# One block of a two-block language model: the overflow branch of its mixture of experts moved to the last expert

## The chip, the cores and the metric

One core of one Trainium2 chip. The time is device microseconds of one execution; of several executions the median is given. The engines are TensorE (PE in the profile; its weight loads are PEld), VectorE (DVE), ScalarE (ACT), GpSimd (POOL) and SyncE (SP), which here only issues DMAs. Each has its own instruction queue and works through it in order; they wait for each other by semaphores.

## The reference

512 tokens of width 1024 go through a first model of two layers (retention and gated linear attention with a SwiGLU, then an HGRN2 mixer with a mixture of experts) and through a second one of one layer. What matters here is the mixture of experts at the end of the first model:

```python
def moe_swiglu(h, w_router, w_gate, w_up, w_down):
    xt = h.reshape(b * t, d)
    logits = (xt @ w_router).astype(jnp.float32)
    top_logits, top_idx = lax.top_k(logits, TOP_K)          # 2 of 8
    gates = jax.nn.softmax(top_logits, axis=-1)
    ...
    hid = (jax.nn.silu(lax.ragged_dot(xs, w_gate, group_sizes))
           * lax.ragged_dot(xs, w_up, group_sizes))
    ys = lax.ragged_dot(hid, w_down, group_sizes)
    ...
    out = jnp.einsum('nk,nkd->nd', gates.astype(y.dtype), y)
```

with 8 experts, each of a gate and an up matrix of 1024 x 3584 and a down matrix of 3584 x 1024 in float32: some 44 MB an expert.

## The kernel before, in words

`build` runs `mixer_ab`, `ffn`, `mixer_c` (first model), `moe`, then `mixer2` and `peer` (second model). The residual `h` stays in SBUF as four tiles of 128 tokens.

**Slots.** Experts are taken in order of how many tokens they have; the place e has a fixed number of slots, `CAPS` = 152, 152, 144, 136, 132, 128, 124, 120. Expert 0 of the weights is always taken first (its key is the largest, from `iota8`), the other places' expert numbers are computed and stand in `eid`. Tokens that find no slot go a second, slower way, `moe_overflow` (L1196): it is a branch on the value `anyo`, and with these inputs it is skipped.

**The entry**, `moe` from L856 on. `moe_ranks` (L1088) takes the router's logits, finds the two best experts of each token, counts with matmuls against a triangular matrix how many tokens stand before it (`pr`, L1111), and works out on VectorE, in some thirty small instructions, the places, the flags `anyo` and `flags`, the overflow rank `rk` and the row `pos` of each token in the DRAM buffer `xg`. Then `values_load` (L878) brings `anyo` into a register of every engine, and `tc.If` (L879) holds the overflow path. `moe_route` (L1178) follows: it makes `first`, for each token tile a 128 x 152 table with the token's scale at its slot with the first expert (L1183; it lies in the tile `hid2`, which the overflow path also writes), scales the token rows (`xn`, L1190), scatters them on POOL to `xg` (eight indirect DMAs, L1065), and computes the gates. `prep_first` (L895) gathers the first expert's tokens by a matmul of `h` with `first` (L900; so it need not wait for the scatters), 8 times over 128 columns, and `split` (L888) makes of each result a high part, a bfloat16 copy (ACT) and a low part (VectorE).

**The experts**, L929 on. Each has 14 chunks of gate and up: `wload_b` (L1052) loads 1 MB on SP (L1055), ACT makes the high part `wh` (L1057), VectorE the low part `wl` (L1058); then per 128 columns a group of 8 matmuls with `wh` (L960) and 8 with `wl` (L962), so four groups a chunk. The down matrix comes in 16 loads (L994, L998). Raw weights lie in five buffers, three of the pool `wraw` and two of a second pool, taken in turn; the overflow path loads its weights into `wraw` too. High and low parts have four buffers, two from each of two pools, which the overflow path does not use. Four PSUM tiles (`mm`) hold the sums until ACT and VectorE have taken them out (L963, L964). The last expert's results are added to `h` at once, with a selection matmul; the others are stored to `yg` by ACT (L1027, L1029) and gathered at the end. `prep(e + 1)` (L904) loads the next expert's token rows from `xg` on ACT's queue (L908, and L911 for the rows beyond 128 where there are any: experts 1 to 4) and transposes them while expert e runs.

**The order in each queue** is not that of the program. The tile framework's scheduler lays the instructions out by program order and by when they will be ready; the whole `tc.If` is placed as one piece, and instructions that share no tile with it may go to either side. `issue_after` puts VectorE instructions behind given ones: here all VectorE work of the first expert behind `first`. A tile name in a pool stands for as many buffers as `bufs` says, used in turn; a new tile waits for the users of the old one, those inside the `tc.If` too.

## Time and profile before

| | us |
|---|---|
| median of 3 runs (lowest, highest) | 3930.39 (3926.33, 3931.0) |
| the profiled execution, its own time | 3932.15 |
| its span, from the first to the last instruction | 3930.4 |
| TensorE busy in the span | 3732.5 (95%) |
| VectorE | 2859.0 (73%) |
| ACT | 2122.3 (54%) |
| mixture of experts, first gather matmul | 1098.07 |
| last expert's first gate and up matmul | 2079.4 |

Mean granted clock of TensorE: 0.969. Times in the views are microseconds from the start of the span. In a timeline a row gives start, duration, engine, line, operation, what is written and read, how many instructions are merged, and in brackets how long the engine had been idle and what ended that. In the table of stretches a row gives the stretch, its length, the busy time (and instructions) of PE, PEld, DVE, ACT and POOL, the granted clock of TensorE as a share of 2.4 GHz, the busy share of the DMA rings and their GB/s. An engine's name with a q (SPq, PEldq) is its queue: DMA issues, branches, register loads and semaphore steps.

### The profile page before, as it was taken

The numbers are of one execution on the slowest core, as the hardware profiler recorded it, in microseconds if no ns is written. First come the engines' busy times: TensorE is split into PE (matmuls) and PEld (weight loads), VectorE is DVE, ScalarE is ACT, GpSimd is POOL, SyncE is SP. The second block draws the span as 40 slices with busy tenths as digits, with TensorE's granted clock in tenths as the row PEclk, the third lists the DMA queues.
The fourth block names the chain that finished last, engine by engine and source line by source line (L and its number), as shares of the span: only waits on it lengthen the run. The fifth ranks groups of instructions, "written<-read, shape, count | busy, mean of one in ns | idle before, by whom it ended". The sixth has DMA issues, their size and how long they took to land.

```text
span 3930.4 us, 64830 instructions
## 1 busy us (share of the span) xinstructions
PE 3732.5 (95%) x25823; PEld 3375.3 (86%) x25824; DVE 2859.0 (73%) x4565; ACT 2122.3 (54%) x3418; POOL 587.0 (15%) x364
## 2 busy tenths in 40 slices
PE   8999999999879999999999799998999899999997
PEld 7887888899879999999999787788999899788886
DVE  4655642545478888999999867569997777677777
ACT  4432222555467877888888565533347676333333
POOL 0000000000010000000000200002335656233333
PEclk9999999999989999999999899899999999999999
DMA  4244542212178888899999521126877777989996
GB/s 141 89 126 169 192 156 92 94 66 70 65 260 310 297 320 325 321 348 343 355 331 370 223 72 42 36 104 227 282 251 248 242 267 260 355 337 334 343 343 226
DMA packets 229131, 887.48 MB, mean 226 GB/s; under 512 B 21080, under 2 KB 81769, under 8 KB 176981
## 3 DMA queue, kind: packets, MB, share of 16 engines
q1 hardware_dynamic: 150706, 640.57, 45.5%
q0 software_dynamic: 40608, 146.29, 10.6%
q10 hardware_dynamic: 37507, 96.42, 6.8%
q8 instruction: 204, 3.34, 0.3%
q14 instruction: 106, 0.87, 0.1%
HBM read 810.11 MB, written 71.47 MB: 224 GB/s over the span
## 4 chain that ended last, share of the span: by engine, by line
PE 45%; DVE 12%; issue 6%; DMA 5%; ACT 2%; POOL 2%; SPq 1%; ACTq 0%; POOLq 0%; DVEq 0%
PE mm L960 8%; PE mm L994 5%; PE acc L165 5%; PE acc L167 5%; PE acc L166 5%; PE mm L962 4%; PE mm L998 2%; DVE wl L160 2%; DVE row L1954 2%; DMA G<-gst 2%; DMA row<-in_peer_u_rows,eidx 1%; DVE wl L1058 1%; PE mm L165 1%; PE mm L167 1%; PE mm L166 1%
## 5 line engine op out<-in xcount | busy, mean ns | idle before, releaser
L1058 DVE TENSOR_TENSOR wl<-wraw,wh 128x2048 bf16<-128x2048 f32 (+1 forms) x352 | 772.1, 2196 | 126.2 <-ACT wh L1057 123.4
L1057 ACT ACTIVATE wh<-wraw 128x2048 fp32r<-128x2048 f32 (+1 forms) x352 | 647.6, 1841 | 174.8 <-PE mm L994 65.3
L160 DVE TENSOR_TENSOR wl<-wraw,wh 128x2048 fp32r<-128x2048 f32 (+1 forms) x219 | 511.1, 2334 | 255.3 <-ACT wh L159 253.8
L159 ACT ACTIVATE wh<-wraw 128x2048 fp32r<-128x2048 f32 (+1 forms) x219 | 415.7, 1898 | 474.3 <-PE mm L166 188.1
L960 PE MATMUL mm<-xhl,wh 128*128 128x304 f32 (+6 forms) x3584 | 566.2, 300 | 14.6 <-DVE gate L964 9.7
L960 PEld LDWEIGHTS mm<-xhl,wh 128*128 128x128 f32 x3584 | 475.7, 190 | 20.7 <-DVE gate L964 7.1
L167 PE MATMUL mm<-xh,wl 128*128 128x384 f32 (+1 forms) x1088 | 376.4, 351 | 19.4 <-DVE wl L160 19.1
L165 PE MATMUL mm<-xh,wh 128*128 128x384 f32 (+1 forms) x1088 | 379.9, 351 | 5.5 <-issue 2.2
L166 PE MATMUL mm<-xl,wh 128*128 128x384 f32 (+1 forms) x1088 | 378.6, 348 | 0.0
L1757 POOL DMA_INDIRECT row<-in_peer_u_rows,eidx x128 | 207.2, 1619 | 594.6 <-DVE pv L1781 405.6
L962 PE MATMUL mm<-xb,wl 128*128 128x152 bf16 (+6 forms) x3584 | 292.3, 224 | 0.0
L166 PE MATMUL acc<-wl,ah 128*128 128x512 f32 x768 | 291.9, 396 | 0.0
L167 PE MATMUL acc<-wh,al 128*128 128x512 f32 x768 | 279.5, 396 | 2.9 <-DVE al L2056 2.9
L165 PE MATMUL acc<-wh,ah 128*128 128x512 f32 x768 | 268.2, 396 | 2.8 <-ACT ah L2055 2.8
L994 PE MATMUL mm<-hid,wh 128*128 128x304 f32 (+6 forms) x1792 | 259.3, 296 | 2.0 <-DVE gate L964 2.0
L1757 POOL DMA_INDIRECT row<-in_peer_v,eidx x128 | 192.9, 1507 | 357.8 <-DVE h L1961 309.2
L994 PEld LDWEIGHTS mm<-hid,wh 128*128 128x128 f32 x1792 | 233.6, 190 | 2.6 <-PE mm L962 2.4
L962 PEld LDWEIGHTS <-wl 128*128 128x128 bf16 x3584 | 212.3, 98 | 26.4
L167 PEld LDWEIGHTS mm<-xh,wl 128*128 128x128 f32 x1088 | 210.6, 194 | 26.7 <-DVE wl L160 23.6
L165 PEld LDWEIGHTS mm<-xh,wh 128*128 128x128 f32 x1088 | 211.8, 195 | 10.9 <-issue 2.8
L166 PEld LDWEIGHTS mm<-xl,wh 128*128 128x128 f32 x1088 | 210.9, 194 | 2.8
L1954 DVE CUSTOM_DVE_ANT_0 row<-row,h 128x1024 f32<-128x1024 f32 x128 | 173.7, 1386 | 44.5 <-DMA row<-in_peer_u_rows,eidx 44.4
(597 smaller groups left out, 8138.5 us busy)
## 6 DMA issues: line engine op xcount, KB each, us to landing
wraw<-in_moe_w_gate SPq DMA_DIRECT2D x112, 1024.0 KB
wraw<-in_moe_w_up SPq DMA_DIRECT2D x112, 1024.0 KB
wraw<-in_moe_w_down SPq DMA_DIRECT2D x128, 896.0 KB
wraw<-in_peer_u SPq DMA_DIRECT2D x64, 1024.0 KB
wraw<-in_peer_v SPq DMA_DIRECT2D x64, 1024.0 KB
wraw<-in_w_ada SPq DMA_DIRECT2D x24, 1024.0 KB
G<-gst SPq DMA_DIRECT2D x24, 1024.0 KB
gw<-G ACTq DMA_DIRECT2D x64, 384.0 KB
```

Of the source, the lines that this page charges most:

```text
L159: nc.scalar.activation(wh[:, :n], raw[:, :n], AF.Copy)
L160: nc.vector.tensor_sub(wl[:, :n], raw[:, :n], wh[:, :n].bitcast(F))
L165: mm(out, ah, bh, start=start, stop=False)
L166: mm(out, ah, bl, start=False, stop=False)
L167: mm(out, al, bh, start=False, stop=stop)
L960: nc.tensor.matmul(ps, wh[:, d, fs], xhl[:, d], start=d == 0, stop=False)
L962: nc.tensor.matmul(ps[:, 0], wl[:, d, fs], xb[:, d], start=False, stop=d == ND - 1)
L994: nc.tensor.matmul(ps, wh[:, fs], hid[at[ft][0]][:, at[ft][1]], start=ft == 0, stop=False)
L1057: nc.scalar.activation(wh[:, :n], raw[:, :n], AF.Copy)
L1058: nc.vector.tensor_sub(wl[:, :n], raw[:, :n], wh[:, :n].bitcast(F))
L1757: self.tc.keep_in_program_order(nc.gpsimd.indirect_dma_start(out=r, out_offset=None, in_=table, in_offset=bass.IndirectOffsetOnAxis(ap=eid ...
L1954: nc.vector.tensor_tensor_reduce(r, r, h2, 1.0, 0.0, op0=OP.mult, op1=OP.add, accum_out=dots[:, q:q + 1])
```

## The change

The `tc.If` with the overflow path goes from the entry to the top of the last expert's turn. In front of it the last expert's first two weight loads are issued and split (`ready`). `b0`, `r0` and `first` are made inside `moe_ranks`, straight behind the counting matmuls, in a tile of their own in the pool `moe` (four times 152 floats a partition). The second row tile of `prep` is named `yr2`, so that it shares one buffer with the output tile of that name, which the overflow path uses too. `of_expert` and the load of the expert's number stand a little higher in the loop.

```diff
@@ -873,12 +873,10 @@
             self.open_w(self.mw)
             rstd = ph.tile([128, NT], F, name="mrstd")
             ranks = self.moe_ranks(ph, psum, flags, anyo, rstd, pos)
+            first = ranks.first
             self.mr.close()
             work = c.enter_context(tc.tile_pool(name="moew", bufs=2, reuse_waits="tile"))
-            rv = nc.values_load(anyo[0:1, 0:1], min_val=0, max_val=1)
-            with tc.If(rv > 0):
-                self.moe_overflow(work, psum, h, g, rstd, ranks, flags, xo, yo, yg)
-            done, first = self.moe_route(ph, work, h, ranks, gates, pos, rstd)
+            self.moe_route(ph, work, h, ranks, gates, pos, rstd)
 
             def parts(C):
                 return (work.tile([128, ND * 2 * CAP], FR, name="xhl")[:, :ND * 2 * C].rearrange(
@@ -907,7 +905,7 @@
                 xr = work.tile([128, D], F, name="xr", bufs=1)[:n]
                 ld = [nc.scalar.dma_start(xr, xg[row:row + n])]
                 if C2:
-                    xr2 = work.tile([CAP - 128, D], F, name="xr2", bufs=1)[:C2]
+                    xr2 = work.tile([CAP - 128, D], F, name="yr2", bufs=1)[:C2]
                     ld.append(nc.scalar.dma_start(xr2, xg[row + n:row + C]))
                 for l in ld:
                     for s in self.scatters:
@@ -923,28 +921,35 @@
                 return x
 
             order = ExitStack()
-            for x in done:
+            for x in ranks.done:
                 order.enter_context(tc.issue_after(x.ins))
             ready = self.ready + [self.wload_b(a[n][0, 1], 2048) for n in ("moe_w_gate", "moe_w_up")]
             nxt = prep_first()
             for e in range(NE):
                 if e == 1:
                     order.close()
+                if e:
+
+                    ev = nc.values_load(self.eid[0:1, e:e + 1], engines=(mybir.EngineType.SP,), min_val=0, max_val=NE - 1)
+
+                def of_expert(name, *at):
+                    if e == 0:
+                        return a[name][(0,) + at]
+                    return a[name][(bass.ds(ev, 1),) + at].rearrange("o p c -> (o p) c")
+
+                if e == NE - 1:
+
+                    ready = [self.wload_b(of_expert(n, 0), 2048) for n in ("moe_w_gate", "moe_w_up")]
+                    rv = nc.values_load(anyo[0:1, 0:1], min_val=0, max_val=1)
+                    with tc.If(rv > 0):
+                        self.moe_overflow(work, psum, h, g, rstd, ranks, flags, xo, yo, yg)
                 C, row = CAPS[e], BASE + START[e]
                 n1, C2 = min(C, 128), max(C - 128, 0)
-                if e:
-
-                    ev = nc.values_load(self.eid[0:1, e:e + 1], engines=(mybir.EngineType.SP,), min_val=0, max_val=NE - 1)
                 xhl, xb = nxt
                 hid = [work.tile([128, n * 2 * CAP], FR, name=f"hid{i}", bufs=1)[:, :n * 2 * C].rearrange(
                     "p (n k c) -> p n k c", n=n, k=2) for i, n in enumerate(HID)]
                 hb = [work.tile([128, n * CAP], BF, name=f"hb{i}", bufs=1)[:, :n * C].rearrange(
                     "p (n c) -> p n c", n=n) for i, n in enumerate(HID)]
-
-                def of_expert(name, *at):
-                    if e == 0:
-                        return a[name][(0,) + at]
-                    return a[name][(bass.ds(ev, 1),) + at].rearrange("o p c -> (o p) c")
                 at = [(i, j) for i, n in enumerate(HID) for j in range(n)]
                 for ch in range(NF // 2):
                     sums = []
@@ -1111,6 +1116,15 @@
                 nc.tensor.matmul(pr[:, t], self.low[:, 0:128] if u == t else self.low[:, 128:256], both[:, u],
                                  start=u == 0, stop=u == min(t, NT - 1))
 
+        b0 = pre.tile([128, NT], F, name="b0")
+        nc.vector.tensor_tensor(b0, both[:, :, 0], rstd, op=OP.mult)
+        r0 = pre.tile([128, NT], F, name="r0")
+        nc.vector.tensor_copy(r0, pr[:, :NT, 0])
+
+        first = pre.tile([128, NT, CAP], F, name="first")
+        done = [nc.vector.tensor_scalar(first[:, t], self.iota_cap, r0[:, t:t + 1], b0[:, t:t + 1],
+                                        op0=OP.is_equal, op1=OP.mult) for t in range(NT)]
+
         key = pre.tile([128, 8], F, name="key")
         nc.vector.scalar_tensor_tensor(key, pr[:, NT], 8.0, after, op0=OP.mult, op1=OP.add)
         sq = [128, 8, 8]
@@ -1152,16 +1166,11 @@
             nc.vector.tensor_tensor(sel, oh, x[:, None].to_broadcast(ohs), op=OP.mult)
             nc.vector.tensor_reduce(out, sel, axis=AX.X, op=OP.add)
 
-        b0 = pre.tile([128, NT], F, name="b0")
-        nc.vector.tensor_tensor(b0, both[:, :, 0], rstd, op=OP.mult)
-        r0 = pre.tile([128, NT], F, name="r0")
-        nc.vector.tensor_copy(r0, pr[:, :NT, 0])
-
         over = pre.tile([128, 2, NT], F, name="over")
         nc.vector.tensor_tensor(over, self.tokrow, p, op=OP.subtract)
         nc.vector.scalar_tensor_tensor(over, rk, 0.0, over, op0=OP.is_ge, op1=OP.mult)
         nc.vector.scalar_tensor_tensor(pos, p, float(BASE), over, op0=OP.add, op1=OP.add)
-        return SimpleNamespace(top=top, idf=idf, rk=rk, b0=b0, r0=r0)
+        return SimpleNamespace(top=top, idf=idf, rk=rk, first=first, done=done)
 
 
     def moe_gates(self, pre, x, rstd, gates):
@@ -1177,20 +1186,14 @@
 
     def moe_route(self, pre, work, h, x, gates, pos, rstd):
         nc = self.nc
-        C = CAP
-
-        first = work.tile([128, HID[2] * 2 * C], F, name="hid2", bufs=1)[:, :NT * C].rearrange("p (t c) -> p t c", t=NT)
-        done = [nc.vector.tensor_scalar(first[:, t], self.iota_cap, x.r0[:, t:t + 1], x.b0[:, t:t + 1],
-                                        op0=OP.is_equal, op1=OP.mult) for t in range(NT)]
         xn = []
         for t in range(NT):
             if t % 2 == 0:
-                xp = work.tile([128, 2 * ND * C], F, name="xhl") if t == 0 else work.tile([128, HID[1] * 2 * C], F, name="hid1", bufs=1)
+                xp = work.tile([128, 2 * ND * CAP], F, name="xhl") if t == 0 else work.tile([128, HID[1] * 2 * CAP], F, name="hid1", bufs=1)
             xn.append(xp[:, (t % 2) * D:(t % 2 + 1) * D])
             nc.vector.tensor_scalar(xn[t], h[:, t], rstd[:, t:t + 1], None, op0=OP.mult)
         self.scatter_rows(self.xg, pos, xn, BASE + START[NE])
         self.moe_gates(pre, x, rstd, gates)
-        return done, first
 
 
     def moe_overflow(self, po, psum, h, g, rstd, x, flags, xo, yo, yg):
```

## Rows read from the trace of the kernel before

**Rows 1.** Stretches of the experts: length, busy us by engine, clock, DMA

```profile
1160.00:1200.00 40.00, 40.00 (x378) 37.99 (x376) 36.74 (x49) 33.77 (x54) 0.00 (x0) 1.00 0.88 308
2064.00:2079.00 15.00, 15.00 (x176) 14.70 (x175) 13.28 (x12) 10.66 (x13) 0.00 (x0) 1.00 0.99 399
2110.00:2160.00 50.00, 49.56 (x551) 47.13 (x551) 47.75 (x70) 44.06 (x79) 0.00 (x0) 1.00 0.97 361
```

**Rows 2.** The same view, stretches of the entry

```profile
1089.00:1098.00 9.00, 0.00 (x0) 0.00 (x0) 4.91 (x28) 1.28 (x1) 0.00 (x0) 0.57 0.02 6
1098.00:1103.00 5.00, 4.39 (x16) 4.05 (x16) 2.93 (x11) 0.00 (x0) 1.75 (x2) 0.50 0.79 246
...
1113.00:1128.00 15.00, 14.09 (x118) 13.31 (x116) 5.10 (x11) 8.11 (x18) 0.79 (x1) 0.96 0.78 312
```

**Rows 3.** Timeline of the entry, TensorE and VectorE

```profile
1088.43 0.49 PE L1111 MATMUL mm<-both,low 128*128 128x8 bf16 x14 [2.28 <-DVE both L1107]
...
1089.04 1.41 DVE L1190 TENSOR_SCALAR xhl<-h,mrstd 128x1024 f32<-128x1024 f32 x2
...
1097.57 1.17 DVE L1183 TENSOR_SCALAR hid<-iotac,r,b 128x152 f32<-128x152 f32 x4 [2.73 <-PEq L879]
...
1098.07 4.39 PE L900 MATMUL tr<-hid,h 128*128 128x152 f32 x16 [9.15 <-DVE hid L1183]
```

**Rows 4.** L878 and L879 on the queues: ns least/median/most, first, last start

```profile
L878 PEldq TENSOR_LOAD <-anyo x1: 490/490/490, 1093.2 to 1093.2; - x1
...
L879 SPq EVENT_SEMAPHORE  x9: 17/17/17, 1096.9 to 1097.5; - x9
...
L879 PEldq COMPARE_BRANCH  x1: 3633/3633/3633, 1093.8 to 1093.8; - x1
```

**Rows 5.** Timeline: expert 0's loads of chunks 3, 1; split; wait

```profile
1045.68 0.33 SPq L1055 DMA_DIRECT2D wraw<-in_moe_w_gate  x1
...
1098.15 0.34 SPq L1055 DMA_DIRECT2D wraw<-in_moe_w_gate  x1
...
1105.11 1.91 ACT L1057 ACTIVATE wh<-wraw 128x2048 fp32r<-128x2048 f32 x1 [9.44 <-DMA wraw<-in_moe_w_gate]
...
1107.06 2.29 DVE L1058 TENSOR_TENSOR wl<-wraw,wh 128x2048 bf16<-128x2048 f32 x1 [5.99 <-ACT wh L1057]
...
1109.69 2.39 PE L900 MATMUL tr<-hid,h 128*128 128x152 f32 x8 [7.23 <-DVE xhl L891]
```

**Rows 6.** Scatters and after: timeline; chain (start, us, what)

```profile
1100.94 1.04 POOL L1065 DMA_INDIRECT xg<-xhl,pos  x1 [413.81 <-DVE selp L1038]
...
1111.77 2.03 POOL L1065 DMA_INDIRECT xg<-hid,pos  x1 [0.30 <-issue]
...
1111.77 13.48 DMA xg<-hid,pos
1125.25 0.03 ACTq L908
...
1127.91 1.40 PE L960 MATMUL mm<-xhl,wh 128*128 128x304 f32 x8 [0.85 <-DVE gate L964]
```

**Rows 7.** Timeline, start of the last expert

```profile
2073.93 0.33 SPq L1055 DMA_DIRECT2D wraw<-in_moe_w_gate  x1
...
2080.82 1.14 PE L960 MATMUL mm<-xhl,wh 128*128 128x240 f32 x8
...
2082.22 1.14 PE L960 MATMUL mm<-xhl,wh 128*128 128x240 f32 x8
...
2084.30 0.25 ACTq L1027 DMA_DIRECT2D yg<-yr  x1
```

**Rows 8.** A wait in the last expert, and the stretch behind it

```profile
2099.38 1.16 PE L960 MATMUL mm<-xhl,wh 128*128 128x240 f32 x8 [2.07 <-DVE w_up L964]
...
2099.30:2105.00 5.70, 5.62 (x45) 5.48 (x46) 5.70 (x10) 4.86 (x9) 2.24 (x1) 0.70 0.96 308
```

**Rows 9.** Timeline: expert 0's store of its rows beyond 128

```profile
1275.90 0.32 ACTq L1029 DMA_DIRECT2D yg<-yr  x1
```

## The prediction

> **What bounds the kernel now.** I read the table of stretches first, for the mixture of experts alone. The reader is to see that TensorE is busy without a gap inside an expert (40.00 of 40 us) and that where the last expert's weights come in, and in its body, VectorE and the DMA rings are nearly full too, with TensorE still at 49.56 of 50 [rows 1]. So whatever the entry saves in front of this stage moves everything behind it forward, and whatever stops TensorE inside it is paid.
>
> The entry is the exception. In the table of its stretches TensorE does nothing from 1089 to 1098, its granted clock is down to 0.50 (the 1.2 GHz level) after that, and only from 1113 is it busy again (14.09 of 15 us). The DMA rings are empty (0.02) just when weights could come in [rows 2].
>
> The timeline then says why. The rank counts leave TensorE at 1088.9 (1088.43 and 0.49). The first expert's slot tables, all that its gather matmul needs beside h, start only at 1097.57, released by TensorE's sequencer at the branch; the gather matmul starts at 1098.07 [rows 3]. The branch itself, on the queue instructions: a register load of 0.49 us and a compare-and-branch of 3.63 us on TensorE's queue; SyncE comes out between 1096.9 and 1097.5 [rows 4]. The second stall follows from the first: the loads of chunk 1 use the three-buffer pool that the overflow path also uses, so they go out at 1098.15, while a load for chunk 3, into the other pool, had gone out at 1045.68. The first is converted at 1105.11, its low part (VectorE, 1107.06, 2.29 us) stands in VectorE's queue ahead of the split of the gathered tokens, and TensorE waits 7.23 us for that split [rows 5].
>
> A third limit lies behind both. The eight scatters of token rows run on POOL from 1100.94 to 1113.8, their last row lands 13.48 us after its issue began, and ACT's load of the next expert's rows waits for that in ACT's own queue, until 1125.25. TensorE runs without a gap from 1127.91 [rows 6].
>
> **The entry: what goes.** The slot tables need the ranks and one small copy, which is there now too; they are moved, not added (four instructions, 1.17 us [rows 3]), and now lie outside the tiles that the overflow path writes. They can start at about 1089.2, or 1090.5 if two token scalings (1.41 us [rows 3]) go first. TensorE needs the first table plus 0.5 us, as now: I take a start of 1090.5, **7.6 us** earlier (bounds 7.0 to 8.9).
>
> The 7.2 us wait is next. After the change chunk 1's loads have no branch in front of them and can land while the rings are empty, so DMA no longer ends this wait; VectorE's backlog does. From 1089 VectorE has what it did in the two stretches to 1103, 4.91 + 2.93 us [rows 2], and two low parts of 2.29: 12.4 us, to about 1101.4 if it never idles. The first gather matmuls (4.39 us [rows 3]) are over at 1094.9. If the split goes to the end of the backlog, TensorE waits 6.5 us, nearly as now; if it slips in at once, nothing is left. The program puts the low parts ahead of the splits, but the trace shows that the order follows readiness (a token scaling at 1089.04 stands behind the branch in the program and ran before it), so I take half: **3.6 us** saved (0 to 7.2).
>
> What is late next is the scatter. Positions come out between 1096.8 (backlog without the low parts) and 1101.4, against 1100.94 now, because fillers that the branch kept away now go between the rank steps. POOL's 12.9 us stay; the landing of the last one, 11.4 us behind its issue now, takes that or any part of it, since the weights that shared the rings are in already. So ACT may be held until 1110 to 1126, where TensorE's work calls for it some 11 us earlier than 1125. I charge **2.2 us** (0 to all that was won). Entry: 7.6 + 3.6 - 2.2 = **9.0 us** (1 to 15).
>
> **The exit: what the moved branch costs.** All of it moves: register loads on five queues, five branches, SyncE's nine and POOL's six semaphore steps. At the entry TensorE had nothing to do; at the start of the last expert it has.
>
> First the hole on TensorE: 0.49 + 3.63 [rows 4], and 0.1 put on for its semaphore steps: **4.2 us**. The stops of the other engines lie beside this hole and I charge them nothing; where that cover is gone, SyncE's, as long as TensorE's to within 0.6 us, costs what the next term has.
>
> Second, weights. Chunk 0 is loaded and split ahead of the branch by the edit (the same two loads and four conversions as now, so no cost), and chunk 1 lies in the pool that the overflow path doesn't use. Chunk 2's loads do use its pool; the one that now goes out at 2073.93 [rows 7] must follow TensorE's pass. By the entry it goes out 0.6 us after the pass, takes 7.0 us to its conversion and 1.9 us there [rows 5]: 9.5 us. TensorE has eight groups of 1.40 us for chunks 0 and 1 [rows 7]. If n of them stand ahead of its branch it waits 9.5 - 1.4 x (8 - n) us. The overflow path reuses the output row tile, whose store is issued at 2084.30, 4.9 us after the last expert's first group, begun at 2079.4 (one period ahead of 2080.82 [rows 7]): three to four groups. With 3.5, the wait is **3.2 us** (0 to 9.5).
>
> Third, the clock. After an idle time of 2.07 us in front of 2099.38 the granted clock averaged 0.70 over the next 5.7 us [rows 8]: 0.30 x 5.7 = **1.7 us** lost. I take that once (0 to twice).
>
> Against this, that same 2.07 us wait for VectorE lies in the last expert now; with TensorE held just before, VectorE catches up: **-2.1 us** (0 to -4, with its clock dip). Exit: 4.2 + 3.2 + 1.7 - 2.1 = **7.0 us** (2 to 17).
>
> [...]
>
> **The shared buffer.** The second row tile of the next expert takes the name of the output tile, to pay for the slot tables' memory. Its load, issued early now, must follow the store at 1275.90 [rows 9], and stands in ACT's queue. What hides it: the tile is for the next expert, and TensorE has four PSUM tiles ahead of ACT. I take 0; gone, the cover would leave up to a landing of 7.0 us in each of three experts, likelier a part: 0 to 3 us.
>
> **The sum.** Against the profiled execution (3932.15 us, span 3930.4): -9.0 + 7.0 + 0 = -2.0, 3930.15. It lies 1.76 above the median of the runs, 3930.39, so the forecast is **3928.4 us**. A measurement of this kernel tells about 0.2%, 7.9 us, from no change.
>
> **The rivals.** *Faster: the entry comes in whole.* The split slips in at once and the scatter lands early (14.8 us), and TensorE branches ahead of the last expert's groups (exit 4.2 + 1.7 - 2.1 = 3.8): -11.0, 3919.4. For it: empty rings, and fillers that ran out of program order. Against it: 12.4 us of VectorE work in the way. Chance 0.27.
>
> *Slower: the last expert starves.* Place: TensorE's queue where chunk 1 ends. If the scheduler fills the wait for the store with all eight groups, TensorE pays the hole and then 9.5 us with nothing to multiply: 4.2 + 9.5 + 1.7 - 2.1 = 13.3. With an entry of 5.0 (7.6 less 2.6 to the scatters): +8.3, 3938.7. From five groups ahead of the branch on, the forecast's 9.0 is used up; from there it decides. For it: the groups are ready and the branch isn't. Against it: the branch precedes them in the program, and its store is out after three to four. Chance 0.20.
>
> [...] Chance 0.08. That the entry does not change at all I count in here: the scatters would then decide alone.
>
> **How the numbers follow.** The forecast has 0.45; with the level rival 0.53 lie within 0.2%, 0.27 faster, 0.20 slower. The range for 8 in 10 goes from a little below the faster rival, 3917, to a little above the slower one with the shared buffer's part, 3941; what is left outside are an entry at its upper end with a free exit, and an entry that saves nothing with a starved exit.
>
> **What would show it.** Right: gather matmul at about 1090 to 1091, chunk 1 loads before 1060, scatters starting between 1097 and 1102, TensorE gapless from 1116 to 1121 instead of 1128; at the last expert one branch of 3.6 us on TensorE, a gap of 4 us and then one of 0 to 5 us that a wh conversion or a load ends, with the clock at half behind it. Wrong: a gather matmul after 1095, ACT held until 1125, a branch over 5 us, gaps at the last expert of over 12 us in sum or under 4, or ACT waits of over 2 us at the row loads of experts 2 to 4.

## The result and the profile after

The changed kernel takes 3959.64 us, median of six executions (before: 3930.69 in the same series). One of the six was disturbed and is left out of the ratio; the other five lie between 3952.38 and 3968.53, with a median of 3955.49. The ratio is 1.0073, 95% interval 1.0052 to 1.0094: slower by 20 to 37 us, outside the predicted range. A second series gave 1.0070 (1.0045 to 1.0095).

I cut both traces at the same marks. **R** is the end of the last rank-count matmul, **M** the end of the seventh expert's last down matmul, **G** the end of the last expert's last gate or up matmul with a high part, **D** the end of its last down matmul with a high part, **X** the first transpose of the second mixer. Two profiles of each kernel (the second ones are experiments e5 and e12) agree to 1 us in R to M and to 2 us in the others, so I use their means:

| us | before | after | difference |
|---|---|---|---|
| start to R | 1088.9 | 1088.2 | -0.7 |
| R to M: entry and seven experts | 990.6 | 987.5 | -3.1 |
| M to G: branch, last expert's gate and up | 85.1 | 98.4 | +13.3 |
| G to D: its down phase | 51.1 | 58.0 | +6.9 |
| D to X | 22.2 | 23.2 | +1.0 |
| X to the end | 1690.9 | 1697.4 | +6.6 |
| span | 3928.7 | 3952.7 | +24.0 |

**The entry** began as the steps had it. The timeline of the changed kernel, TensorE and ACT's queue:

```profile
1090.73 4.42 PE L898 MATMUL tr<-first,h 128*128 128x152 f32 x16 [1.92 <-DVE first L1125]
1097.81 2.40 PE L898 MATMUL tr<-first,h 128*128 128x152 f32 x8 [2.66 <-DVE xhl L889]
1128.09 0.44 PE L917 MATMUL tr<-c_ident,xr 128*128 128x128 f32 x2 [2.66 <-DMA xr<-xg]
...
1278.82 0.32 ACTq L909 DMA_DIRECT2D yr<-xg  x1
...
1432.69 0.28 PE L919 MATMUL tr<-c_ident,yr 8*128 8x8 f32 x2 [2.17 <-DMA yr<-xg]
```

The gather matmul starts at 1090.73, the wait for the split is 2.66 us in place of 7.23 [rows 5]. Two waits are new: for the next expert's rows (2.66), and at the third expert for the rows in the shared buffer, whose load now goes out behind the store, shortly before it is used (2.17). In between TensorE stands twice more in this profile, 1.99 us in front of 1111.97, for nothing that the profile shows, and 2.07 us in front of 1114.87, for a second split. In the second profile (e12) these two are not there, and the wait for the next expert's rows is 3.78 us.

**The exit** did not. What the branch line did on each queue (ns least/median/most, first and last start):

```profile
L944 SPq EVENT_SEMAPHORE  x9: 17/17/17, 2067.7 to 2088.4; - x9
...
L944 ACTq EVENT_SEMAPHORE  x2: 17/17/17, 2087.8 to 2087.9; - x2
...
L944 PEldq COMPARE_BRANCH  x1: 3616/3616/3616, 2077.9 to 2077.9; - x1
L944 ACTq COMPARE_BRANCH  x1: 58/58/58, 2079.2 to 2079.2; - x1
```

TensorE's branch takes 3.62 us as before [rows 4] and is over at 2081.8. But ACT, which branched at 2079.2, comes out only at 2087.8, and SyncE's last steps end at 2088.4. In the timeline:

```profile
2078.03 0.25 ACTq L1032 DMA_DIRECT2D yg<-yr  x1
...
2087.85 2.06 PE L965 MATMUL mm<-xhl,wh 128*128 128x240 f32 x8 [10.17 <-ACTq L944]
...
2088.70 0.34 SPq L1060 DMA_DIRECT2D wraw<-in_moe_w_gate  x1
...
2091.08 0.28 DVE L969 TENSOR_TENSOR gate<-mm,gate 128x120 f32<-128x120 f32 x1 [11.26 <-ACT gate L968]
2095.34 2.29 DVE L1063 TENSOR_TENSOR wl<-wraw,wh 128x2048 bf16<-128x2048 f32 x1 [3.98 <-ACT wh L1062]
...
2209.28 1.28 DVE L1090 SCALAR_TENSOR_TENSOR h<-xhl,gates,h 128x1024 f32<-128x1024 f32 x1 [9.39 <-DMA xhl<-yg,pos]
```

The store of the seventh expert's rows goes out just ahead of the branch. TensorE stands for 10.17 us, released by ACT's queue at the branch; the first load behind it, chunk 1's, follows at 2088.70. Later VectorE waits 9.39 us for gathered rows. The table of stretches (length, busy us by engine in the order PE, PEld, DVE, ACT, POOL, then clock, DMA share, GB/s), first while only that store moved, then M to G and G to D:

```profile
2078.20:2087.90 9.70, 0.05 (x1) 0.05 (x1) 1.22 (x4) 0.00 (x0) 0.00 (x0) 0.54 0.20 57
...
2076.67:2175.11 98.44, 82.82 (x886) 76.99 (x885) 79.86 (x120) 72.87 (x121) 2.65 (x3) 0.93 0.87 333
2175.11:2233.82 58.71, 46.88 (x504) 45.10 (x504) 49.28 (x48) 33.85 (x42) 20.21 (x12) 0.91 0.80 295
```

and the same two stretches of the kernel before:

```profile
2079.62:2164.73 85.11, 81.98 (x897) 78.16 (x896) 81.64 (x122) 71.84 (x123) 6.50 (x3) 0.98 0.97 365
2164.73:2216.66 51.93, 47.08 (x499) 46.09 (x498) 48.50 (x48) 30.69 (x37) 19.82 (x12) 0.93 0.82 317
```

VectorE does the same work in both, 130.1 and 129.1 us from M to D. Before it was idle 6.9 us of the 137.0, after 28.0 of 157.2, and the three rows shown above (11.26, 3.98, 9.39) are most of it. TensorE's idle time grew nearly as much, from 8.0 to 27.4 us, so these sums do not say which engine the time was lost at; the waits do. In M to G it is the hole, through which both engines stand. In G to D TensorE waits for the low parts of the down matrix, which VectorE makes, before and after:

```profile
L998 PE MATMUL mm<-hb,wl 128*128 128x120 bf16 x213 | 14.1, 217 | 3.6 <-DVE wl L1058 3.6
```

```profile
L1003 PE MATMUL mm<-hb,wl 128*128 128x120 bf16 x210 | 14.3, 222 | 10.4 <-DVE wl L1063 10.4
```

These are groups of instructions from G to D: count, busy time and mean ns of one, then the idle time in front of them and what ended it. The 6.8 us more are the whole growth of this stretch between these two profiles; the second profiles have 8.8 against 3.2.

### The profile page after: what moved, and what is told of

Read it like the earlier page. It is cut to its first block, busy times and chain, and to the rows that moved or that the text cites. A ratio compares the mean times of both kernels' runs of the same rounds, so it can differ in the third digit from the quotient of the medians.

```text
span 3953.7 us, 64889 instructions
## 1 busy us (share of the span) xinstructions
PE 3744.1 (95%) x25823; PEld 3383.6 (86%) x25824; DVE 2853.4 (72%) x4565; ACT 2124.3 (54%) x3417; POOL 563.1 (14%) x364
## 3 DMA queue, kind: packets, MB, share of 16 engines
q0 software_dynamic: 40608, 146.29, 10.5%
## 5 line engine op out<-in xcount | busy, mean ns | idle before, releaser
L1063 DVE TENSOR_TENSOR wl<-wraw,wh 128x2048 bf16<-128x2048 f32 (+1 forms) x352 | 770.9, 2192 | 124.4 <-ACT wh L1062 122.1
L965 PE MATMUL mm<-xhl,wh 128*128 128x304 f32 (+6 forms) x3584 | 563.3, 300 | 20.9 <-ACTq L944 10.2
L965 PEld LDWEIGHTS mm<-xhl,wh 128*128 128x128 f32 x3584 | 476.8, 191 | 25.4 <-ACTq L944 10.4
L167 PE MATMUL mm<-xh,wl 128*128 128x384 f32 (+1 forms) x1088 | 377.7, 352 | 21.7 <-DVE wl L160 21.6
L1760 POOL DMA_INDIRECT row<-in_peer_v,eidx x128 | 177.7, 1388 | 371.0 <-DVE h L1964 321.8
```

Of the source, the lines that this page charges most:

```text
L167: mm(out, al, bh, start=False, stop=stop)
L965: nc.tensor.matmul(ps, wh[:, d, fs], xhl[:, d], start=d == 0, stop=False)
L1063: nc.vector.tensor_sub(wl[:, :n], raw[:, :n], wh[:, :n].bitcast(F))
L1760: self.tc.keep_in_program_order(nc.gpsimd.indirect_dma_start(out=r, out_offset=None, in_=table, in_offset=bass.IndirectOffsetOnAxis(ap=eid ...
```

## The experiments

All with the marks above; lines move by a few between kernels. The ratio is to the kernel before on the same chip.

| kernel | R to M | M to G | G to D | D to X | VectorE idle, M to D | ratio (95%) |
|---|---|---|---|---|---|---|
| before | 990.7 | 85.1 | 51.9 | 22.2 | 6.9 | |
| e5 before again | 990.5 | 85.1 | 50.2 | 22.2 | 5.5 | 1.0005 (0.9990 to 1.0019) |
| after | 987.9 | 98.4 | 58.7 | 23.2 | 28.0 | 1.0073 (1.0052 to 1.0094) |
| e12 after again | 987.1 | 98.4 | 57.3 | 23.2 | 26.5 | 1.0070 (1.0045 to 1.0095) |
| e1 before, no branch | 978.8 | 85.1 | 51.1 | 22.2 | 6.1 | 0.9992 (0.9976 to 1.0008) |
| e2 after, no branch | 984.8 | 83.5 | 52.0 | 22.4 | 6.6 | 0.9990 (0.9975 to 1.0004) |
| e3 branch at expert 5 | 1001.7 | 83.7 | 49.0 | 22.9 | 3.8 | 1.0017 (1.0002 to 1.0033) |
| e4 store behind | 980.2 | 98.7 | 47.3 | 23.8 | 16.7 | 0.9996 (0.9982 to 1.0011) |
| e6 branch behind gather | 993.3 | 83.5 | 52.7 | 22.2 | 7.2 | 1.0024 (1.0012 to 1.0036) |
| e7 tables only | 990.5 | 85.1 | 50.6 | 22.2 | 5.6 | 1.0001 (0.9991 to 1.0011) |
| e8 e4 + chunk 1 raw | 980.1 | 99.2 | 55.0 | 22.8 | 25.7 | 1.0019 (1.0005 to 1.0033) |
| e9 branch only, store behind | 978.8 | 98.4 | 47.6 | 23.6 | 16.4 | 0.9992 (0.9979 to 1.0005) |
| e10 e4 + chunk 1 split | 977.2 | 98.3 | 55.4 | 22.8 | 25.2 | 1.0009 (0.9995 to 1.0023) |
| e11 store on POOL | 986.2 | 90.0 | 58.9 | 23.2 | 19.6 | 1.0014 (1.0000 to 1.0028) |
| e13 after, less VectorE | 982.8 | 98.6 | 43.3 | 20.2 | 38.3 | one time, 3935.2 us |
| e14 e2, less VectorE | 991.7 | 83.5 | 40.5 | 20.8 | 23.8 | one time, 3923.2 us |
| e15 store split | 987.2 | 93.1 | 57.4 | 23.2 | 21.3 | 1.0039 (1.0026 to 1.0053) |

### Repeats: how far a profile can be trusted

e5 is the kernel before and e12 the changed kernel, both without any edit.

> The kernel before, word for word, profiled a second time, to see how far stages of one and the same program differ between two executions. If stages repeat, the stretch from the last rank count to the end of the seventh expert's down matmuls is within 1 us of 990.7, and the attention part of the second mixer within 2 us of 72.0; then differences of 3 to 12 us between the kernels in these stretches are their own. If they don't repeat, by 5 us or more, single profiles can't carry terms of a few us. Time within 0.2% of before.

> The changed kernel, word for word, a second time. Theory one, the 10 us beyond the stages are scatter: time 3950 to 3955, ratio to before 1.005 to 1.006, and the attention part of the second mixer, 77.9 us in the first profile, lies between 71 and 82 at random. Theory two, they are the kernel's own: ratio 1.007 or more again, and the stretch behind the second mixer's first transpose is 5 us or more longer than the 1690 us of the kernel before. In both, the idle time of TensorE at the branch is 10 us again and the stretch from the seventh expert's end to the last down matmul within 2 us of 157.2.

R to M repeats to 0.3 and 0.8 us for one and the same program. Between programs whose edits change no work between R and M it does not: e4 takes 980.2 and e13 982.8 where the changed kernel takes 987.9, and e14 991.7 where e2 takes 984.8. So 5 to 8 us there can't be put down to an edit by one profile. The hole repeated (10.14 us in e12), and M to D is 155.7 us against 157.2. The loss that repeats is 24 us: the five executions of the first series have a median 24.8 us above that of before, the second series has 3954.1 against 3929.9, and the spans differ by 24.0. In this theory two of e12 holds: its ratio is 1.0070, and the stretch behind X takes 1696.6 and 1698.2 us against 1691.5 and 1690.3 (its time lies in theory one's band as well). Most of the 6.6 us behind X is the attention part of the second mixer, here as stretches of before, before again, after, after again:

```profile
2443.61:2515.65 72.04, 64.93 (x334) 48.32 (x335) 37.81 (x138) 43.23 (x117) 0.00 (x0) 0.80 0.01 4
```

```profile
2440.74:2514.62 73.88, 66.28 (x334) 49.98 (x334) 37.90 (x138) 43.15 (x117) 0.00 (x0) 0.76 0.01 4
```

```profile
2460.55:2538.42 77.87, 70.64 (x335) 52.38 (x335) 37.83 (x138) 43.71 (x117) 0.00 (x0) 0.72 0.01 3
```

```profile
2458.26:2535.96 77.70, 70.74 (x334) 52.74 (x334) 37.94 (x138) 43.33 (x117) 0.00 (x0) 0.71 0.01 3
```

The work is the same (same counts of instructions, VectorE 37.8 to 37.9 us); TensorE's granted clock is lower, 0.72 and 0.71 against 0.80 and 0.76, and the stretch 4.8 us longer on the mean. In the other kernels it lies between 71.5 and 81.4 us: 71.6 in e4 at a clock of 0.78, 81.4 in e2 at 0.68. Why the clock there is lower behind one kernel than behind another stays open.

### The hole: what the engines wait for

> The changed kernel with the seventh expert's output rows stored behind the branch and not in front of it (the overflow path uses other tiles for its own). Theory one, the engines come out of the branch only when that store, 496 KB on ACT's queue and about 9.5 us long, has landed: the idle time of TensorE in front of the last expert falls from 10.2 us to 4 to 5 us, ACT comes out within 1.5 us of its branch, and the time falls by 5 to 6 us, to about 3954, or further if the gathers move too. Theory two, it is the instruction fetch: idle time of TensorE still 9 to 11 us, time within 2 us of 3959. Against a gain: the store then lands later, and the last expert's gathers read it.

```diff
                 with tc.If(rv > 0):
                     self.moe_overflow(...)
+                nc.scalar.dma_start(yg[row:row + n1], yr[:n1])
...
-                if not last:
+                if e < NE - 2:
                     nc.scalar.dma_start(yg[row:row + n1], yr[:n1])
```

(The overflow path's `opos` and output tile get other tiles.) Its timeline:

```profile
2058.24 0.34 SPq L1061 DMA_DIRECT2D wraw<-in_moe_w_gate  x1
...
2068.87 0.49 ACTq L946 DMA_DIRECT2D yg<-yr  x1
2069.15 0.33 SPq L1061 DMA_DIRECT2D wraw<-in_moe_w_gate  x1
...
2069.55 2.03 PE L966 MATMUL mm<-xhl,wh 128*128 128x240 f32 x8 [4.65 <-PEq L944]
```

Theory one: the hole is 4.65 us, released by TensorE's own queue, and SyncE is through early, so chunk 1's first load goes out at 2058.24, 11 us ahead of the first group. That the hole goes with the store is shown; that the engines wait for its landing is not (see the end of this section). One figure was a miss: ACT came out 3.1 us behind its branch (2065.5 to 2068.6), not within 1.5. And the gain is not where I put it. M to G is 98.7 us, no better than the changed kernel's 98.4: chunk 2's loads still wait for TensorE's pass (2069.15), now share the rings with the store, and TensorE starves in small pieces. The load of 2069.15 lands 10.5 us after its issue; in the changed kernel the first load behind the branch (2088.70) took 4.7 us, in e11 5.4. What shrinks is G to D, by 10.7 us, because VectorE no longer waits for gathered rows there. The ratio falls to 0.9996; 10.5 us of it is M to D. R is 4.5 us earlier and R to M 7.3 us shorter, although up to the branch PE's, ACT's and VectorE's programs hold the same instructions in the same order as in the changed kernel; why is open, and no part of my reading rests on it.

> The changed kernel with the seventh expert's output rows stored in front of the branch by POOL's queue and not by ACT's. Theory one, each engine waits at the branch only for what its own queue has in flight, so ACT, VectorE and TensorE come out within 1.5 us of their branches and TensorE's hole is 4.6 to 6.5 us, as with the store behind; only the gathers wait. Theory two, SyncE waits for every transfer in flight wherever it was issued, and TensorE for it: hole still 10 us or more. Time 3935 to 3945 by the first (the gathers still late), 3959 by the second.

```diff
-                nc.scalar.dma_start(yg[row:row + n1], yr[:n1])
+                q = nc.gpsimd if e == NE - 2 else nc.scalar
+                q.dma_start(yg[row:row + n1], yr[:n1])
```

```profile
2080.51 2.03 PE L965 MATMUL mm<-xhl,wh 128*128 128x240 f32 x8 [4.47 <-PEq L944]
...
2199.36 1.28 DVE L1091 SCALAR_TENSOR_TENSOR h<-xhl,gates,h 128x1024 f32<-128x1024 f32 x1 [9.28 <-DMA xhl<-yg,pos]
```

Theory one by the hole: with the store on POOL's queue TensorE stands 4.47 us and M to G is 90.0, only 4.9 over before; the rows come late all the same (9.28, G to D 58.9). The time, 3933.8 us, is a little under its band, but the kernel before took 3934.2 in that series; and ACT came out 3.1 us behind its branch (2076.7 to 2079.8), not within 1.5. The hole belongs to the store on ACT's queue, and so does the slow refill behind the branch in e4.

Why 9.5 us for 496 KB? While it moved alone the rings were at a share of 0.20 and 57 GB/s. At the fifth expert (e3) a store of 128 rows in front of the branch moved at up to 420 GB/s, and TensorE stood only 5.16 us. The steps by which a store's semaphore reported its pieces differ as well. In the changed kernel, without the first jump that some of them have, it is 16 for each store of 128 rows, 12 for 24 rows, 16 for 16, 8 for 8 and four for the 124 rows (2085.41 to 2088.18); the 124 rows had four in the kernel before, too. The share of 0.20, near four sixteenths, fits that. By these counts 112 rows, seven times 16, should go in 16 steps and move like the 128: an estimate. So the last test:

> The changed kernel with the seventh expert's store of 124 rows issued as 112 and 12 rows, nothing else. Theory one, the 124 rows are spread over a quarter of the rings (share 0.19 while it moved alone, against 0.6 to 0.99 for the 128 rows at the fifth expert), and 112 rows are spread over all: the store lands within 5 us, ACT comes out of the branch before TensorE does, TensorE's hole is 5 to 6.5 us as with the store behind, and from the seventh expert's end to the last down matmul it takes 146 to 152 us in place of 156 to 157. Theory two, the place or the write itself makes it slow: hole 10 us again, 156 us.

```diff
-                nc.scalar.dma_start(yg[row:row + n1], yr[:n1])
+                for r0, r1 in ((0, 112), (112, n1)) if e == NE - 2 else ((0, n1),):
+                    nc.scalar.dma_start(yg[row + r0:row + r1], yr[r0:r1])
```

```profile
2082.76 2.06 PE L965 MATMUL mm<-xhl,wh 128*128 128x240 f32 x8 [5.39 <-ACTq L944]
...
2086.00 0.28 DVE L969 TENSOR_TENSOR gate<-mm,gate 128x120 f32<-128x120 f32 x1 [6.49 <-ACT gate L968]
...
2202.31 1.28 DVE L1091 SCALAR_TENSOR_TENSOR h<-xhl,gates,h 128x1024 f32<-128x1024 f32 x1 [8.12 <-DMA xhl<-yg,pos]
```

The hole falls from 10.17 to 5.39 us and M to G to 93.1; M to D is 150.5 us, in the expected band, and the ratio 1.0039. From 2078.20 to 2082.70 the rings are at 0.40 and 120 GB/s. ACT was still the releaser, a detail that I had the other way. The rows' wait stays (8.12): the store's landing is not what makes it. In e4, where the first gathers went out later, 18.5 us behind M (12.7 in the changed kernel, 23.1 before), it is not there, so the start of the gathers is not what makes it either. What differs is the order in the down phase. POOL in the changed kernel and then before:

```profile
2190.44 1.85 POOL L1084 MEMSET xhl<- 128x1024 f32 x2 [9.42 <-DVE h L1090]
2192.44 8.13 POOL L1085 DMA_INDIRECT xhl<-yg,pos  x1 [0.15 <-POOL xhl L1084]
```

```profile
2176.60 1.85 POOL L1079 MEMSET xhl<- 128x1024 f32 x2 [6.41 <-DVE h L1085]
```

The gather that VectorE waits for goes out at 2192.44. Its buffer could be cleared only behind VectorE's third row addition, POOL took 8.13 us over it, and its last row landed 16.8 us after the issue. e12, e11 and e15 have the same order and the same 8.1 us; before, in e4 and in e9 the clear follows the second addition. What sets this order I did not test.

What ACT waits for at the branch is less clear than that the store makes the hole. In the changed kernel the store's last piece lands at 2088.18, 0.4 us behind ACT's own steps (2087.78 and 2087.87; the same 0.4 in e12); only a step of SyncE, at 2088.20, follows the landing. What comes ahead of ACT is an instruction transfer of 8 KB, at 2086.23. The DMA queues from 2086 to 2087:

```profile
q10 hardware_dynamic: 9, 0.03, 8.8%
q14 instruction: 1, 0.01, 1.9%
```

From 2079.6 to 2086.2, nearly all the time since ACT's branch, q14 had moved none. In e15 its packet comes at 2081.15, and ACT is out 1.5 us later as here. So the order of these times speaks for a wait for that packet, which came late among the store's pieces, rather than for their landing. That is a reading: no run separates the two.

### The place of the branch

> The changed kernel with the branch in front of the fifth expert in place of the eighth, with that expert's first two weight tiles loaded ahead of it in the same way. Theory one, the branch costs the same anywhere among the experts (hole and refill of the weight buffers, some 10 us): 3927.5 + 10.5 = 3938. Theory two, the last expert is the dear place, because its gathers, row additions and weights all queue behind the branch at once: the same 3938, but then the changed kernel's other 21 us are that place's. Rival, the whole 32 us are the price of a branch among the experts wherever it stands: about 3959.

```diff
-                if e == NE - 1:
+                if e == 4:
...
```

3938.1 us, as theories one and two had it. R to M is 16.9 us over the kernel without a branch (e2), although TensorE's hole is 5.16 us: VectorE stands for 9.5 and 4.4 us there. No gathers hang on it, so nothing is added behind M.

> The changed kernel with the branch back at the entry, but behind the first expert's gather matmul and the issue of the scatters, in front of the first expert's body. Theory one, a branch costs what the busiest engine has to stop for, and weights lie ready there while TensorE waits for splits anyway: a hole of 4 to 5 us on TensorE, two chunks of weights ready behind it, stretch from ranks to the end of the seventh expert 2 to 6 us over the 984.8 us without a branch, time 3930 to 3934. Theory two, the branch waits for whatever transfers are in flight, here the eight scatters and chunk 1's weights: a hole of 10 us or more, time 3938 or above.

```diff
             nxt = prep_first()
+            rv = nc.values_load(anyo[0:1, 0:1], min_val=0, max_val=1)
+            with tc.If(rv > 0):
+                self.moe_overflow(...)
...
```

(The same lines go from the top of the last expert's turn, and here as in e3 the list of scatters is kept over the branch.)

```profile
1112.65 2.37 PE L967 MATMUL mm<-xhl,wh 128*128 128x304 f32 x8 [5.58 <-DVEq L930]
1127.71 2.39 PE L967 MATMUL mm<-xhl,wh 128*128 128x304 f32 x8 [6.26 <-DVE gate L971]
```

Between the theories: the hole is 5.58 us, but a second stop of 6.26 follows, R to M is 8.5 us over e2 and the ratio 1.0024. The old place was the cheaper one.

### The entry

> The kernel before without the branch and the path for overflowing tokens (that path is left out), everything else as it was. It prices the branch at the entry alone. My prediction's entry account says it gives 9.0 us: about 3921.5 us against 3930.5. The rival, that the scatters and the row loads behind them decide when TensorE runs again and the branch only stood beside them, says about 3 us or less: 3927.5 to 3930.5. The trace of the changed kernel, 2.9 us ahead at the end of the seventh expert, speaks for the rival.

> The changed kernel without the branch and the overflow path (left out); the slot tables stay straight behind the ranks and the last expert's first weights stay where they are. Theory one, the whole loss lies behind the moved branch: it comes out 2.9 us under before, as the changed kernel stands at the end of the seventh expert, so about 3927.5, and the moved branch costs 32 us. Theory two, a part of the loss is the new order in the last expert or in the second mixer and not the branch: it comes out above 3931, by up to 15 us (the 17 to 23 us of lag in those stages less the 8.4 us at the first group).

Both edits take the three lines of the `tc.If` away. R to M falls by 11.8 us in e1, where the slot tables stay late, and by 5.8 in e2, where they are early and the buffer is shared. By the stages the branch did hold the entry, in e1 by more than my 9.0, with the 5 to 8 us of scatter between programs said above; by the times, 0.9992 and 0.9990, it is nearer to the rival's 3 us (the intervals reach to 9 or 10 us of gain). In both profiles the stretch behind X is long, 1703.7 and 1701.7 us against 1690.9, of which the attention part is 78.3 and 81.4; the two profiled executions took 3936.0 and 3933.6 us, above the medians of their series. For the sum of the loss this means theory one of e2: behind the branch.

> The changed kernel with the branch at its old place, straight behind the ranks, so that only the slot tables are made earlier. If the branch alone held the entry, the early tables bring nothing: gather matmul still 8 to 9 us behind the last rank count (9.15 before), time 3928 to 3933. If the tables themselves were what the gather waited for, it comes 1 to 3 us earlier.

With the early tables alone, branch at its old place, the gather matmul starts 10.2 us behind the last rank count and nothing moves: R to M 990.5, ratio 1.0001.

> The branch in front of the last expert with the store behind it, but the slot tables made where the kernel before makes them, behind the token scalings, and the second row tile in a buffer of its own again. So of the change only the branch is moved. Theory one, the early tables and the shared buffer give nothing once the branch is gone from the entry, and cost something: ranks to the end of the seventh expert is 978 to 980 us, as without any branch (978.8), and no wait for the second row tile at the start of the third and fourth experts; time 3928 to 3932. Theory two, the early tables are what fills TensorE at the entry: the stretch comes out 3 us or more above the 980.2 of the kernel with both.

Theory one: R to M is 978.8, to 0.1 us that of e1. From R to the first down matmul of the first expert (before, after, e9):

```profile
1088.92:1218.15 129.23, 111.94 (x976) 105.16 (x977) 100.00 (x162) 91.56 (x158) 10.71 (x8) 0.91 0.81 287
```

```profile
1088.81:1216.41 127.60, 116.30 (x977) 108.88 (x977) 99.82 (x162) 87.25 (x155) 7.84 (x8) 0.91 0.74 264
```

```profile
1081.84:1201.07 119.23, 109.75 (x977) 102.92 (x977) 99.48 (x162) 86.63 (x155) 7.83 (x8) 0.96 0.79 284
```

The changed kernel idles 6.0 us less than before (11.3 for 17.3), but its granted clock is 0.91 all the same, so the same matmuls take 4.4 us more. e9 idles 9.5 us at a clock of 0.96. With the early tables the entry's idle time lies in short pieces, and the second eight gather matmuls take 2.40 us where e9 has 1.30. But the stage varies: 124.4 us at a clock of 0.92 in the second profile of the changed kernel, 123.0 in e4 and 121.4 in e10, all with early tables, 120.3 in e1 without. The fair pair is e4 and e9, which differ in the tables and the row buffer alone: 1.4 us in R to M, and times of 0.9996 and 0.9992. So the early tables give nothing, and that they cost something is not shown.

### The refill

> The kernel with the store behind the branch, and with the raw loads of the last expert's chunk 1 issued in front of it as well (they lie in the pool that the overflow path doesn't use). Theory one, behind the branch TensorE is fed by loads that can't be issued earlier, so two loads in flight across it save a good part of the refill: hole and body of gate and up fall from 98.7 us to 90 to 94 (83.5 without a branch), time about 3925. Theory two, the branch waits until these two loads have landed too: hole over 6 us, time 3931 or above. Theory three, VectorE's conversions and not the loads set the refill: 98 us again, time unchanged.

> The kernel with the store behind the branch, and chunks 0 and 1 of the last expert both loaded and converted in front of it (four tile pairs where the change has two). Theory one, what is paid behind the branch is the idle time of VectorE, which is nearly full in the last expert: two more low parts of 2.29 us done in front of the branch give that much back; hole and body fall from 98.7 us to 93 to 95. Theory two, TensorE starves for weights until chunk 2 has come in (9.5 us from SyncE's issue to the split), and two chunks ready, 11.2 us of groups, cover that: 88 to 91 us. Theory three, neither, 98 us, as with the raw loads alone (99.2). Time: the same amount under the 3931.5 of the kernel without it.

e8 issues the two raw loads of chunk 1 in front of the branch, e10 makes `ready` of chunks 0 and 1. Neither helps M to G (99.2 and 98.3): a miss for theory one in both. The timeline of e10:

```profile
2064.14 0.34 SPq L1061 DMA_DIRECT2D wraw<-in_moe_w_gate  x1
...
2074.46 1.91 ACT L1063 ACTIVATE wh<-wraw 128x2048 fp32r<-128x2048 f32 x1 [6.83 <-DMA wraw<-in_moe_w_gate]
...
2078.94 2.07 PE L966 MATMUL mm<-xhl,wh 128*128 128x240 f32 x8 [5.69 <-DVE gate L970]
```

Chunk 2's load, in the pool that the overflow path uses, goes out at 2064.14, behind the branch, and is converted 10.3 us later; by then TensorE's eight groups are through and it stands 5.69 us. In e4 chunk 1 was issued early anyway. So it is chunk 2 that sets the refill, and what lies ready before it only moves the stop. In all four kernels with the store behind the branch (e4, e8, e9, e10) this load shares the rings with the 124 rows and takes 9.8 to 10.7 us to land; with the store on POOL's queue it took 5.4, and M to G was 90.0. The slow store costs in front of the branch, by the hole, or behind it, by the refill. A store behind the branch and split into 112 and 12 rows I did not try. G to D grows (55.0 and 55.4): VectorE waits 6.76 us for gathered rows in e10.

### VectorE relieved

> The changed kernel with the low parts of the last expert's down weights left out (sixteen VectorE conversions of 2.03 us, and the 224 bf16 matmuls that read them, some 12.6 us of TensorE). Against its pair without the branch. Theory one, VectorE's idle time is what is paid: with 32 us less work it can stand still for the rows without holding TensorE, and the price of the branch from the seventh expert's end to the last down matmul falls from 21.7 us to 16 or less, all of it in hole and gate and up (15 us). Theory two, late weights and rows themselves hold the down phase: the price stays at 20 us or more.

> The pair of it: the changed kernel without branch and overflow path (left out), and without the low parts of the last expert's down weights (left out). From the seventh expert's end to the last down matmul 122 to 128 us in place of 135.5, since TensorE has 12.6 us less and the rings, busy for 125 us of it, come near; VectorE's busy time there 97 us in place of 129.

The two stretches M to G and G to D, e13 and then e14:

```profile
2071.90:2170.54 98.64, 83.08 (x886) 77.23 (x885) 79.85 (x120) 72.84 (x121) 2.67 (x3) 0.93 0.87 332
2170.54:2213.82 43.28, 35.51 (x297) 33.14 (x298) 23.77 (x38) 33.45 (x44) 12.53 (x12) 1.00 0.98 400
```

```profile
2079.92:2163.44 83.52, 80.92 (x898) 76.77 (x897) 79.07 (x123) 71.55 (x124) 6.08 (x3) 1.00 0.97 361
2163.44:2203.93 40.49, 34.07 (x289) 32.31 (x287) 21.11 (x34) 30.79 (x40) 11.52 (x12) 1.00 0.97 404
```

e14 lies in its band (124.0 us; VectorE busy for 100.2). The branch costs 141.9 - 124.0 = 17.9 us here, against 21.7 with all the work: between the two theories' bounds. Its parts: in G to D the price falls from 6.7 to 2.8 us, which fits VectorE's stops being what was paid there, but the edit also takes 12.6 us of work from TensorE, and each of the two kernels has a single time; in M to G it stays at 15.1, where TensorE, VectorE and the rings (0.97) are all near full and stop together.

## Why the prediction was wrong

**The step that failed** is in the exit: "The stops of the other engines lie beside this hole and I charge them nothing". At the entry they did lie beside it, when hardly anything was in flight (DMA share 0.02 [rows 2]). At the last expert the store that I had read in rows 7 as a mark of time only was moving, at 57 GB/s; ACT came out 8.6 us behind its branch, where it had taken 0.5 at the entry, and TensorE stood until it was out. That made the hole 10.17 us where I had 4.2. With the store behind the branch it is 4.65 (e4), on POOL's queue 4.47 (e11), in two pieces 5.39 (e15), so the 4.2 was about right for the branch alone. Rows 7 said when the store went out, and I never asked how long it would move.

**The second miss** is a term that I did not have: 6.9 us in the down phase. VectorE, which I had read as nearly full in the body [rows 1], waits 9.39 us there for gathered rows, and TensorE waits 10.4 us for its low parts in place of 3.6. The branch did not hold the gathers back: the first goes out at 2089.32, 12.7 us behind M, and before at 23.1. The row additions and buffer clears come in another order than before, and why is open. I had VectorE as full and still priced only TensorE.

**The rest of the exit** was about right in its sum, in part by luck: starvation 3.2, clock 1.7, recovered -2.1 make 2.8 us; M to G less the hole shows 13.3 - 11.4 = 1.9 (the hole taken from M, 11.2 us against -0.2). But the steps were other ones. I had three to four groups ahead of TensorE's branch, and there were none; in the changed kernel chunk 1's loads, too, went out only behind the branch (2088.70). And in e4, where the hole is nearly as I had it, M to G is still 13.6 us over before, so there these terms come to 9 us and not 2.8. That chunk 2's loads must follow TensorE's pass is what e4, e8 and e10 show.

**The entry** gave 3.1 us to the end of the seventh expert, where the sum had 9.0 (bounds 1 to 15). The first two terms held: 7.2 us for 7.6 at the gather, 4.6 for 3.6 at the split (3.0 against the second profile of before). The give-back was put at 2.2 and comes to 8.7 by the same sum: rows 2.66 us late, two stops of some 2 us that only one profile has, and the half clock (0.50 from 1090.73 to 1095.15, over the first gather matmuls), which I had charged at the exit but not here; with R to M 5 to 8 us apart between programs of the same work, its parts are not shown. The shared buffer, taken as 0 with a bound of 3, cost a wait of 2.17 us (2.79 in e12). In e9, where only the branch is moved, the stage is 11.8 us shorter than before, with the same scatter.

**The rivals.** The faster one's entry of 14.8 us came in nowhere: the most is 13.4 (e10), then 11.8 (e1 and e9). The slower one, "the last expert starves", has 13.3 us for its exit, which is what M to G shows, but not by its mechanism: TensorE had no groups ahead of its branch to use up, and stood until ACT was out. The level one, with its 0.08, rested on a branch that takes longer the fuller the rings are. No run shows that term for TensorE: its branch took 3.62 us, as before, with the rings at 0.17 to 0.20, and in e3, with the store moving at up to 420 GB/s, 4.38; no run here had a branch under rings that stayed full. On ACT, where I did not look, it was 8.6 us from the branch to the next step, with the instruction packet late; that other traffic made it late is a reading of these traces.

**What beats the kernel before**: none beyond the measurement. Of the kernels that keep the overflow path e9, the branch moved with the store behind it and the tables left late, comes nearest (0.9992, 0.9979 to 1.0005).

## What to carry to other kernels

A branch among full engines was priced here by what each engine waited for (10.17 us on TensorE), not by the branch instruction (3.62 us): look up which transfers are moving when the engines reach it, and how long they move. Where several engines were near full, their stops showed up as idle time of all of them (21 us on VectorE and 19 on TensorE), so look at what each wait is for and not at the sums. And of a change with two parts, try each alone: here the early tables gave nothing by themselves (e7), and without them the moved branch did as well (e9).

## What the runs showed of the hardware

A store of 124 rows and 496 KB moved at 57 GB/s, and TensorE stood 10.17 us at the branch behind it; with the store issued as 112 and 12 rows it stood 5.39. A 1 MB load issued while such a store moved landed after 9.8 to 10.7 us, and after 4.7 to 5.4 as the first behind the branch without it. TensorE's branch took 3.62 us (the changed kernel), 3.63 (before), 3.75 (e11), 3.86 (e4) and 4.38 (e3); ACT's own branch instruction took 0.06, but its next step came 0.5 us (before) to 8.6 us behind it (the changed kernel). One and the same attention stage took 71.5 to 81.4 us in the kernels tried: 72.0 at a granted clock of TensorE of 0.80, 77.9 at 0.72, 81.4 at 0.68; that is as much as most edits here are worth.
